# Attention output and expert queries: one block at a time, or two blocks on each weight tile

## The chip, the cores and the metric

The kernel runs on one core of a Trainium2 chip. The metric is device time in microseconds (us). An execution has five engines that run their own instruction lists in order, each list fixed when the kernel is built: TensorE (PE, with its weight loads as PEld), VectorE (DVE), ScalarE (ACT), GpSimd (POOL) and SyncE (SP), whose queue issues almost all plain transfers. Indirect transfers (gathers) are issued by POOL.

## The reference

Two layers over 512 tokens of width 1024, all in f32, with six modulation vectors per layer that are computed from a condition `c`.

```python
for l in range(DEPTH):
    mod = c_act @ ada_w[l] + ada_b[l]                      # [1024] x [1024, 6144]
    sh1, sc1, g1, sh2, sc2, g2 = jnp.split(mod, 6, axis=-1)
    h = _modulate(x, sh1, sc1)
    mix = _hybrid_mixer(h, ...)                            # h @ w_in [1024, 1952], three kinds of heads, @ w_o [1024, 1024]
    x = _layer_norm(alpha * x + (1.0 + g1) * mix, ln1_g[l], ln1_b[l])
    h = _modulate(x, sh2, sc2)
    ffn = _peer(h, peer_wq[l], peer_k1[l], peer_k2[l], peer_u[l], peer_v[l])
    x = _layer_norm(alpha * x + (1.0 + g2) * ffn, ln2_g[l], ln2_b[l])
```

The mixer is causal over the tokens: a block of 128 tokens attends to itself and to the blocks ahead of it. `_peer` multiplies h by `wq` [1024, 2048], scores the result against two sets of 128 keys in each of 8 heads, takes the best 16 of each set, the best 16 of the 256 sums, and so 128 experts of 16384 for each token. Each expert is a row of 1024 in `u_tab` and one in `v_tab`: `out = sum(g * gelu(u . h) * v)`.

## The kernel before, in words

The tokens are four blocks of 128 (0 to 3). A layer has two stages.

**Attention stage.** For each block: `prepare` (layer norm, transpose to `hT`), `project` (times w_in, for a pair of blocks at once), `attend` (the three kinds of heads, result `cat`), `output` (times w_o, result `rt`), `between` (row operations with the modulation rows, layer norm, the new residual `xs`, the second modulation `h2d`, its transpose `h2T`), `queries` (times peer_wq in four groups of 512 columns; for each group a copy, transposes `ptq`, key scores `pms`, a copy `scs`, and the best 16 on DVE, L617 to L622), and `pick`, which ends in the expert numbers `eidx` (L669). The weight products all go through `gemm` (L149 to L162). A weight tile `wt` is 512 KB: four row groups of 128 by 256 columns. SP issues its load when one of 3 or 4 buffers is free. `output` and `queries` are called for one block, so w_o and peer_wq are read four times a layer. `project` is called for (0, 1) and (2, 3), so w_in is read twice.

In the order of the code, blocks 0 and 1 go through attend, output, between, queries and pick one after the other. `project` of (2, 3) is held behind the last query matmul of block 0 (`behind`). Block 2 then attends; the second half of its queries stands behind block 3's attention.

`ada_side` computes the modulation vectors beside layer 0's attention: 20 groups of 512 columns, each from 256 KB tiles `adw` in three buffers. For the first eight groups DVE multiplies and adds (L207, L209); for the last twelve, half of the columns goes over ACT (L203) and POOL (L205). A small matmul `adp` (L211) sums each half over the partitions.

**Expert stage.** For blocks 1 and 2 all experts are computed: the tables u and v are streamed through PE in full (`dense`), after DVE and PE have built a matrix G from the picks of both blocks (`build`, DVE lines L788 to L797, PE L804). Blocks 0 and 3 gather their own experts (`experts`): POOL issues a gather of 128 rows, 512 KB, and DVE multiplies it, L696 and L698 for u, L708 and L713 for v. Four gather buffers exist, so a gather waits until DVE is done with the gather four before. `EARLY` gathers, 80 in layer 0 and 110 in layer 1, have no place ordered for them; they may go out as soon as block 0 has its `eidx`. The later gathers are tied to steps of the build and of the dense loop. Four more go out with the first build steps, so 84 and 114 gathers are issued ahead of the build. The last 50 of layer 0 stand in layer 1's attention.

A list scheduler sets the order of each engine's instructions when the kernel is built, from a model of their times. So a late instruction on an engine holds all that stands behind it there.

## Time and profile before

| | |
|---|---|
| median of three runs | 3564.16 us (3544.61 to 3568.53) |
| the profiled execution | 3550.53 us, of which the span is 3548.8 us |
| busy: PE, DVE, POOL, ACT | 87%, 78%, 42%, 26% of the span |
| moved by DMA | 1012.14 MB, 285 GB/s on the mean |
| granted TensorE clock, mean | 0.927 of full speed |
| layer 0: attention stage until the first build step | 0 to 676.1 us |
| layer 1: attention stage until the first build step | to 2427.1 us |

The dense stage takes the rest: from 676.1 to about 1780 us, and from 2427.1 us to the end. In f32 each matmul is two records in the trace. The weight loads are 128 of peer_wq, 64 of w_o and 56 of w_in, of up to 512 KB each. Rows that name L157 are the matmuls of `gemm`; h2T, cat or hT beside it tells whether they belong to queries, output or projection.

### The profile page before, as it was taken

The numbers are of one execution on the slowest core, as the hardware profiler recorded it, in microseconds if no ns is written. First come the engines' busy times: TensorE is split into PE (matmuls) and PEld (weight loads), VectorE is DVE, ScalarE is ACT, GpSimd is POOL, SyncE is SP. The second block draws the span as 40 slices with busy tenths as digits, with TensorE's granted clock in tenths as the row PEclk, the third lists the DMA queues.
The fourth block names the chain that finished last, engine by engine and source line by source line (L and its number), as shares of the span: only waits on it lengthen the run. The fifth ranks groups of instructions, "written<-read, shape, count | busy, mean of one in ns | idle before, by whom it ended". The sixth has DMA issues, their size and how long they took to land.

```text
span 3548.8 us, 54489 instructions
## 1 busy us (share of the span) xinstructions
PE 3072.0 (87%) x19708; PEld 2258.0 (64%) x19708; DVE 2765.7 (78%) x6277; ACT 927.4 (26%) x1860; POOL 1476.2 (42%) x1347
## 2 busy tenths in 40 slices
PE   7889768658999999999948896776699999999998
PEld 4657536536777776777736774555467767777775
DVE  4668996999777877776675579889998778776777
ACT  2342432222222222222222223312222222222221
POOL 1025573256343334444462045534454434444543
PEclk9989889859999999999979996997699999999998
DMA  9777978568898888899986586885789988989997
GB/s 276 221 230 251 313 261 287 174 187 282 306 322 307 316 310 310 311 348 344 337 288 206 173 292 211 296 294 178 238 275 350 333 312 316 331 323 335 358 353 256
DMA packets 430173, 1012.14 MB, mean 285 GB/s; under 512 B 40504, under 2 KB 229192, under 8 KB 429904
## 3 DMA queue, kind: packets, MB, share of 16 engines
q0 software_dynamic: 147456, 536.94, 42.5%
q1 hardware_dynamic: 282448, 471.73, 39.6%
q8 instruction: 156, 2.56, 0.3%
q14 instruction: 113, 0.93, 0.1%
HBM read 1002.06 MB, written 6.34 MB: 284 GB/s over the span
## 4 chain that ended last, share of the span: by engine, by line
PE 13%; DVE 13%; DMA 10%; issue 9%; POOL 4%; ACT 1%; SPq 0%; POOLq 0%; DVEq 0%; ACTq 0%
DMA g<-in_peer_v,eidx 5%; PE pm L157 4%; PE acc L849 3%; DVE acc L713 2%; POOL g L696 2%; DVE g L698 2%; DMA g<-in_peer_u,eidx 2%; DVE tk_ef L668 1%; PE sp L831 1%; PE sp L832 1%; PE sp L833 1%; PE utp L817 1%; DMA wt<-in_peer_wq 1%; POOL g L708 1%; DVE o L797 1%
## 5 line engine op out<-in xcount | busy, mean ns | idle before, releaser
L708 POOL DMA_INDIRECT g<-in_peer_v,eidx x512 | 613.4, 1198 | 782.0 <-DVE acc L713 481.7
L849 PE MATMUL acc<-v,ge 128*128 128x512 f32 x2048 | 928.9, 595 | 6.4 <-DVE ge L837 5.8
L696 POOL DMA_INDIRECT g<-in_peer_u,eidx x512 | 603.2, 1178 | 764.4 <-DVE g L698 499.9
L713 DVE SCALAR_TENSOR_TENSOR acc<-g,wts,acc 128x1024 f32<-128x1024 f32 x508 | 674.2, 1327 | 145.1 <-DMA g<-in_peer_v,eidx 137.7
L698 DVE SCALAR_TENSOR_TENSOR g<-g,h 128x1024 f32<-128x1024 f32 x512 | 620.3, 1225 | 172.9 <-DMA g<-in_peer_u,eidx 161.8
L831 PE MATMUL sp<-hh,uh 128*128 128x256 f32 x2048 | 613.7, 300 | 1.6 <-ACT ge L835 0.9
L849 PEld LDWEIGHTS acc<-v,ge 128*128 128x128 f32 x2048 | 370.3, 190 | 370.7 <-issue 364.1
L833 PE MATMUL sp<-hh,ul 128*128 128x256 f32 x2048 | 594.8, 290 | 0.0
L832 PE MATMUL sp<-hl,uh 128*128 128x256 f32 x2048 | 583.7, 285 | 0.0
L819 ACT CAST uh<-utp 128x512 fp32r<-128x512 f32 x512 | 304.1, 595 | 871.9 <-PE utp L817 710.9
L821 DVE TENSOR_TENSOR ul<-utp,uh 128x512 fp32r<-128x512 f32 x512 | 347.6, 684 | 110.5 <-ACT uh L819 104.2
L831 PEld LDWEIGHTS sp<-hh,uh 128*128 128x128 f32 x2048 | 392.4, 192 | 7.6 <-issue 5.5
L832 PEld LDWEIGHTS sp<-hl,uh 128*128 128x128 f32 x2048 | 392.1, 191 | 5.3 <-issue 5.3
L833 PEld LDWEIGHTS sp<-hh,ul 128*128 128x128 f32 x2048 | 391.4, 191 | 0.1
L817 PE MATMUL utp<-ident,u 128*128 128x128 f32 x2048 | 302.9, 277 | 49.0 <-DVE ul L821 46.5
L817 PEld LDWEIGHTS utp<-ident,u 128*128 128x128 f32 x2048 | 236.4, 142 | 126.9 <-issue 70.7
L806 ACT COPY G<-pg 128x344 f32<-128x344 f32 (+1 forms) x192 | 146.8, 765 | 593.9 <-PE pg L804 477.5
L804 PEld LDWEIGHTS <-o 128*128 128x128 bf16 x4608 | 163.3, 102 | 187.4 <-issue 91.9
L804 PE MATMUL pg<-o,o 128*128 128x43 bf16 (+1 forms) x4608 | 183.9, 190 | 104.7 <-DVE o L797 86.4
L157 PE MATMUL pm<-wt,h2T 128*128 128x256 f32 x1024 | 235.9, 385 | 17.6 <-DMA wt<-in_peer_wq 16.7
L157 PE MATMUL pm<-wt,hT 128*128 128x256 f32 (+1 forms) x1024 | 232.4, 380 | 12.6 <-ACT hT L274 6.3
L157 PEld LDWEIGHTS pm<-wt,h2T 128*128 128x128 f32 x1024 | 193.3, 193 | 51.0 <-DMA wt<-in_peer_wq 21.5
(235 smaller groups left out, 3448.2 us busy)
## 6 DMA issues: line engine op xcount, KB each, us to landing
u<-in_peer_u SPq DMA_DIRECT2D x256, 512.0 KB
v<-in_peer_v SPq DMA_DIRECT2D x256, 512.0 KB
wt<-in_peer_wq SPq DMA_DIRECT2D x128, 512.0 KB
adw<-in_ada_w SPq DMA_DIRECT2D x160, 256.0 KB
wt<-in_w_o SPq DMA_DIRECT2D x64, 512.0 KB
wt<-in_w_in SPq DMA_DIRECT2D x56, 512.0 KB
wt<-in_ada_w SPq DMA_DIRECT2D x16, 512.0 KB
g<-in_peer_u,eidx POOLq DMA_INDIRECT x512
```

The source lines that it names most:

```text
L157: r = nc.tensor.matmul(pm[:, c0:c0 + m], lhsT=lhsT[:, k0 + k, :], rhs=wt[:, k, :m], start=k0 + k == 0, stop=k0 + k == KT - 1)
L696: nc.gpsimd.indirect_dma_start(out=g, out_offset=None, in_=u_flat, in_offset=bass.IndirectOffsetOnAxis(ap=eidx[:, h, k:k + 1], axis=0))
L698: after(nc.vector.scalar_tensor_tensor(out=g, in0=g, scalar=1.0, in1=h2, op0=OP.mult, op1=OP.mult, accum_out=dots[:, h, k:k + 1]))
L708: nc.gpsimd.indirect_dma_start(out=g, out_offset=None, in_=v_flat, in_offset=bass.IndirectOffsetOnAxis(ap=eidx[:, h, k:k + 1], axis=0))
L713: r = nc.vector.scalar_tensor_tensor(out=acc, in0=g, scalar=wts[:, h, k:k + 1], in1=acc, op0=OP.mult, op1=OP.add)
L804: nc.tensor.matmul(pg[:, tt, 0:n], lhsT=o2[:, tt // TI, :, tt % TI], rhs=o1a[:, tt // TI, p, 0:n, tt % TI], start=tt == 0 and p == 0, stop ...
L817: nc.tensor.transpose(pt[:, j * P:(j + 1) * P], u[:, k * P:(k + 1) * P], ident)
L821: nc.vector.tensor_tensor(ul.rearrange("p j t -> p (j t)"), pt, uh.rearrange("p j t -> p (j t)").bitcast(F32), op=OP.subtract)
L831: nc.tensor.matmul(sp, lhsT=uh[:, j, :], rhs=hh[:, k, :], start=k == 0, stop=False)
L832: nc.tensor.matmul(sp, lhsT=uh[:, j, :], rhs=hl[:, k, :], start=False, stop=False)
L833: nc.tensor.matmul(sp, lhsT=ul[:, j, :], rhs=hh[:, k, :], start=False, stop=k == KT - 1)
L849: nc.tensor.matmul(acc[i][g], lhsT=w[:, i * P:(i + 1) * P], rhs=v[:, g * 512:(g + 1) * 512], start=a == 0, stop=a == NK - 1)
```

## The change

`gemm` takes tiles of two row groups by 512 columns instead of four by 256; a tile stays 512 KB, and a row of it in memory is 2 KB instead of 1 KB. `output` and `queries` take a list of two blocks, and each tile serves both. So w_o is loaded 32 times instead of 64 and peer_wq 64 instead of 128, 48 MB less in all. The products are the same. The order of the stage changes with it: both blocks of a pair attend, then comes one output for both, the two `between`, one `queries` for both, and the two picks. `project` of (2, 3) is held behind the last query matmul of blocks 0 and 1. The pick of block 2 follows the queries of blocks 2 and 3. `ada_side` works on tiles of 128 by 512, and DVE's operations there are 512 columns wide for the first eight groups. Buffers: weight tiles of layer 0 from 4 + 3 to 3 + 3, of layer 1 from 4 + 4 to 4 + 3; the tiles `rt`, `h2d`, `h2T` from 2 to 3; the transposes and scores of the queries take their PSUM tiles from the tag of the transposes ("tr").

```diff
--- before.py
+++ after.py
@@ -35,12 +35,11 @@
...
-WK = 4
-ADK = 2
+WK = 2
...
-BUFS = (dict(w=4, wp=3, scs=1), dict(w=4, wp=4, scs=2))
+BUFS = (dict(w=3, wp=3, scs=1), dict(w=4, wp=3, scs=2))
@@ -147,18 +146,16 @@
...
     def gemm(src, n, lhsTs, pms, tag, behind=None):
-        for c0 in range(0, n, 256):
-            m = min(256, n - c0)
-            for k0 in range(0, KT, WK):
-                wt = A.w.tile([P, WK, 256], F32, name="wt", tag=tag, bufs=A.bufs[tag])
-                nc.sync.dma_start(wt[:, :, :m], src[k0 * P:(k0 + WK) * P, c0:c0 + m].rearrange("(k p) n -> p k n", p=P))
-                for lhsT, pm in zip(lhsTs, pms):
-                    for k in range(WK):
-                        r = nc.tensor.matmul(pm[:, c0:c0 + m], lhsT=lhsT[:, k0 + k, :], rhs=wt[:, k, :m],
-                                             start=k0 + k == 0, stop=k0 + k == KT - 1)
-                        if behind is not None:
-                            order(r, behind)
-                            behind = None
+        for k0 in range(0, KT, WK):
+            wt = A.w.tile([P, WK, 512], F32, name="wt", tag=tag, bufs=A.bufs[tag])
+            nc.sync.dma_start(wt[:, :, :n], src[k0 * P:(k0 + WK) * P, :].rearrange("(k p) n -> p k n", p=P))
+            for lhsT, pm in zip(lhsTs, pms):
+                for k in range(WK):
+                    r = nc.tensor.matmul(pm[:, :n], lhsT=lhsT[:, k0 + k, :], rhs=wt[:, k, :n],
+                                         start=k0 + k == 0, stop=k0 + k == KT - 1)
+                    if behind is not None:
+                        order(r, behind)
+                        behind = None
         return r
...
     def ada_side(l, groups):
         for g in groups:
             t = A.ad.tile([P, 512], F32, name="adt", bufs=1)
-            for c0 in range(0, 512, 256):
-                tt = t[:, c0:c0 + 256]
-                for q in range(0, KT, ADK):
-                    wt = A.ad.tile([P, ADK, 256], F32, name="adw", bufs=3)
-                    nc.sync.dma_start(wt, ada_w[l, q * P:(q + ADK) * P, g * 512 + c0:g * 512 + c0 + 256]
-                                      .rearrange("(k p) n -> p k n", p=P))
-                    for k in range(ADK):
-                        ck = cact[:, q + k:q + k + 1]
-                        if l and c0 == 0:
-                            w = tt if q == 0 and k == 0 else wt[:, k, :]
-                            nc.scalar.activation(w, wt[:, k, :], AF.Copy, scale=ck)
-                            if q or k:
-                                nc.gpsimd.tensor_tensor(tt, tt, w, op=OP.add)
-                        elif q == 0 and k == 0:
-                            nc.vector.tensor_scalar(tt, wt[:, k, :], ck, None, op0=OP.mult)
-                        else:
-                            nc.vector.scalar_tensor_tensor(tt, wt[:, k, :], ck, tt, op0=OP.mult, op1=OP.add)
+            for k in range(KT):
+                wt = A.ad.tile([P, 512], F32, name="adw", bufs=3)
+                nc.sync.dma_start(wt, ada_w[l, k * P:(k + 1) * P, g * 512:(g + 1) * 512])
+                ck = cact[:, k:k + 1]
+                m = 256 if l else 0
+                if m:
+                    w = t if k == 0 else wt
+                    nc.scalar.activation(w[:, 0:m], wt[:, 0:m], AF.Copy, scale=ck)
+                    if k:
+                        nc.gpsimd.tensor_tensor(t[:, 0:m], t[:, 0:m], wt[:, 0:m], op=OP.add)
+                if k == 0:
+                    nc.vector.tensor_scalar(t[:, m:], wt[:, m:], ck, None, op0=OP.mult)
+                else:
+                    nc.vector.scalar_tensor_tensor(t[:, m:], wt[:, m:], ck, t[:, m:], op0=OP.mult, op1=OP.add)
...
-    def output(y, b, cat):
+    def output(y, cats):
         l = y.l
-        rt = A.work.tile([P, D], F32, name="rt", tag="tok", bufs=2)
+        rts = [A.work.tile([P, D], F32, name="rt", tag="tok", bufs=3) for _ in cats]
         for c0 in range(0, D, 512):
-            pm = A.ps.tile([P, 512], F32, name="pm", tag="mm", bufs=2)
-            gemm(w_o[l, :, c0:c0 + 512], 512, [cat], [pm], "w")
-            nc.scalar.copy(rt[:, c0:c0 + 512], pm)
-        return rt
+            pms = [A.ps.tile([P, 512], F32, name="pm", tag="mm", bufs=2) for _ in cats]
+            gemm(w_o[l, :, c0:c0 + 512], 512, cats, pms, "w")
+            for rt, pm in zip(rts, pms):
+                nc.scalar.copy(rt[:, c0:c0 + 512], pm)
+        return rts
...
-        h2 = A.work.tile([P, D], F32, name="h2d", tag="tok", bufs=2)
+        h2 = A.work.tile([P, D], F32, name="h2d", tag="tok", bufs=3)
...
-    def queries(y, h2T, v1, fi, groups):
+    def queries(y, hs):
         l = y.l
-        for g in groups:
-            pm = A.ps.tile([P, 512], F32, name="pm", tag="mm", bufs=2)
-            r = gemm(peer_wq[l, :, g * 512:(g + 1) * 512], 512, [h2T], [pm], "w")
...
+        for g in range(4):
+            pms = [A.ps.tile([P, 512], F32, name="pm", tag="mm", bufs=2) for _ in hs]
+            r = gemm(peer_wq[l, :, g * 512:(g + 1) * 512], 512, [h[0] for h in hs], pms, "w")
+            qs = []
+            for pm in pms:
+                q = A.work.tile([P, 512], F32, name="q", tag="q", bufs=2)
+                nc.scalar.copy(q, pm)
+                qs.append(q)
+            for q, (_, v1, fi) in zip(qs, hs):
+                pt = A.ps.tile([P, 512], F32, name="ptq", tag="tr", bufs=2)
+                for m in range(4):
...
+                kT = A.work.tile([P, 4, P], F32, name="qkT", tag="qkT", bufs=1)
...
+                pm = A.ps.tile([P, 4, NK], F32, name="pms", tag="tr", bufs=2)
...
+                top16([(v1[:, 4 * g + m, :], i1[:, m, :], scs[:, m, :]) for m in range(4)])
+                nc.vector.tensor_copy(fi[:, 2 * g:2 * g + 2].rearrange("p h a k -> p (h a) k"), i1)
         return r
@@ -914,31 +912,26 @@
         if l + 1 < L:
             ada_side(0, range(4, 12))
         layer_rows(y)
-        behind = None
         for p in ps:
-            b = p[0]
             attend(y, *p)
-            if b == 1:
-                for b2 in (2, 3):
-                    prepare(y, b2)
-            h = between(y, b, output(y, b, p[2]))
-            r = queries(y, *h, range(4))
-            if b == 0:
-                behind = r
+        for b in (2, 3):
+            prepare(y, b)
+        rts = output(y, [p[2] for p in ps])
+        hs = [between(y, b, rt) for b, rt in zip((0, 1), rts)]
+        behind = queries(y, hs)
+        for b, h in zip((0, 1), hs):
             res[b] = pick(b, *h[1:])
-        p2, p3 = project(y, (2, 3), behind)
+        ps = project(y, (2, 3), behind)
         if l + 1 < L:
             ada_side(1, range(12))
-        attend(y, *p2)
-        h = between(y, 2, output(y, 2, p2[2]))
-        queries(y, *h, range(2))
-        attend(y, *p3)
-        rt = output(y, 3, p3[2])
-        queries(y, *h, range(2, 4))
-        res[2] = pick(2, *h[1:])
-        h = between(y, 3, rt, lambda: A.ps.tile([P, 512], F32, name="prow", tag="at", bufs=2))
-        queries(y, *h, range(4))
-        res[3] = partial(pick, 3, *h[1:])
+        for p in ps:
+            attend(y, *p)
+        rts = output(y, [p[2] for p in ps])
+        mk = lambda: A.ps.tile([P, 512], F32, name="prow", tag="at", bufs=2)
+        hs = [between(y, b, rt, mk) for b, rt in zip((2, 3), rts)]
+        queries(y, hs)
+        res[2] = pick(2, *hs[0][1:])
+        res[3] = partial(pick, 3, *hs[1][1:])
```

Where the change moves instructions: PE in layer 0, at the end of the queries of the first block. In these rows `pm<-wt,h2T` are query matmuls, `pm<-wt,hT` is the projection of blocks 2 and 3, `pm<-wt,cat` the output of block 1, `ptq` and `pms` the transposes and scores of the queries, `prow` the modulation rows of a `between`. Before:

```order
L157 MATMUL pm<-wt,h2T 128x256 x12
L211 MATMUL adp<-adt,nones 1x512
L157 MATMUL pm<-wt,h2T 128x256 x4
L157 MATMUL pm<-wt,hT 128x256 x11
L601 MATMUL ptq<-ident,q 128x128 x4
L157 MATMUL pm<-wt,hT 128x256 x5
L157 MATMUL pm<-wt,hT 128x160 x6
L606 MATMUL pms<-keysT,qkT 128x128 x4
L157 MATMUL pm<-wt,cat 128x256 x16
L157 MATMUL pm<-wt,hT 128x160 x4
L157 MATMUL pm<-wt,cat 128x256 x8
L227 LDWEIGHTS sel
```

The projection, the output of block 1 and its `between` stand mixed with the queries. With the change, at the start of the queries of blocks 0 and 1:

```order
L220 MATMUL prow<-rows_159,sel 128x256
L258 MATMUL pt<-ident,h2d 128x128 x8
L204 MATMUL adp<-adt,nones 1x512
L154 MATMUL pm<-wt,h2T 128x512 x12
L204 MATMUL adp<-adt,nones 1x512
L154 MATMUL pm<-wt,h2T 128x512 x4
L599 MATMUL ptq<-ident,q 128x128 x4
L154 MATMUL pm<-wt,h2T 128x512 x8
L604 MATMUL pms<-keysT,qkT 128x128 x4
L599 MATMUL ptq<-ident,q 128x128 x4
L154 MATMUL pm<-wt,h2T 128x512 x4
```

Here all `prow` and both transposes of h2d stand ahead of the first query matmul, and no `hT` or `cat` matmul stands among the queries; the projection follows as a whole behind the last of them.

POOL in layer 0, around block 2's `between`: `ve` and `rs_r` are the two small steps of a layer norm on POOL, two pairs for each `between`; L696 and L708 (L694 and L706 with the change) are block 0's gathers. Before:

```order
L708 DMA g<-in_peer_v,eidx_1674 128x1024
L205 TENSOR_TENSOR adt<-adt,adw 128x256
L708 DMA g<-in_peer_v,eidx_1674 128x1024 x3
L248 TENSOR_SCALAR ve<-bnmv 128x1
L237 TENSOR_TENSOR rs_r<-ve,mhalf 128x1
L708 DMA g<-in_peer_v,eidx_1674 128x1024 x3
L248 TENSOR_SCALAR ve<-bnmv 128x1
L237 TENSOR_TENSOR rs_r<-ve,mhalf 128x1
L708 DMA g<-in_peer_v,eidx_1674 128x1024
L696 DMA g<-in_peer_u,eidx_1674 128x1024
L205 TENSOR_TENSOR adt<-adt,adw 128x256 x3
L696 DMA g<-in_peer_u,eidx_1674 128x1024
```

The `between` of block 2 stands among the last of the first 32 v gathers; the next 20 u gathers and block 3's `between` follow. With the change, at the same place:

```order
L706 DMA g<-in_peer_v,eidx_1943 128x1024 x2
L665 TENSOR_TENSOR tk_pick<-tk_hot,tk_ce 128x400
L706 DMA g<-in_peer_v,eidx_1943 128x1024 x29
L694 DMA g<-in_peer_u,eidx_1943 128x1024 x20
L241 TENSOR_SCALAR ve<-bnmv 128x1
L230 TENSOR_TENSOR rs_r<-ve,mhalf 128x1
L241 TENSOR_SCALAR ve<-bnmv 128x1
L230 TENSOR_TENSOR rs_r<-ve,mhalf 128x1
L241 TENSOR_SCALAR ve<-bnmv 128x1
L230 TENSOR_TENSOR rs_r<-ve,mhalf 128x1
L241 TENSOR_SCALAR ve<-bnmv 128x1
L230 TENSOR_TENSOR rs_r<-ve,mhalf 128x1
```

All 84 gathers now stand ahead of the two `between` of blocks 2 and 3. In layer 1 it is the same with 114.

## Rows read from the trace of the kernel before

**Rows 1.** the page, part 1: busy us, share of the span, instructions

```profile
PE 3072.0 (87%) x19708; PEld 2258.0 (64%) x19708; DVE 2765.7 (78%) x6277; ACT 927.4 (26%) x1860; POOL 1476.2 (42%) x1347
```

**Rows 2.** stretches: length, busy us (instructions) by engine, clock, DMA share, GB/s

```profile
0.00:50.00 50.00, 34.19 (x136) 12.82 (x136) 17.57 (x59) 7.94 (x8) 9.53 (x22) 0.97 1.00 300
...
200.00:210.00 10.00, 4.26 (x11) 1.63 (x11) 10.00 (x21) 1.35 (x3) 1.64 (x4) 0.50 0.25 80
...
210.00:220.00 10.00, 10.00 (x51) 7.84 (x52) 4.40 (x9) 9.63 (x26) 3.28 (x6) 0.78 0.45 142
...
350.00:400.00 50.00, 45.78 (x218) 34.76 (x216) 44.69 (x178) 16.86 (x38) 23.78 (x25) 1.00 1.06 374
...
450.00:500.00 50.00, 34.79 (x116) 20.23 (x114) 47.23 (x62) 13.65 (x28) 38.72 (x37) 0.80 0.73 235
...
650.00:700.00 50.00, 28.39 (x286) 24.55 (x287) 48.03 (x166) 14.92 (x27) 14.17 (x15) 0.80 0.41 141
...
1500.00:1700.00 200.00, 200.00 (x1115) 145.05 (x1115) 139.99 (x193) 43.84 (x85) 89.53 (x77) 1.00 0.94 347
```

**Rows 3.** lines 0 to 690 us: count, busy us, mean ns, idle before, releasers

```profile
L157 PE MATMUL pm<-wt,h2T 128*128 128x256 f32 x512 | 118.1, 386 | 7.9 <-DMA wt<-in_peer_wq 7.6 <-issue 0.4
...
L157 PE MATMUL pm<-wt,hT 128*128 128x256 f32 (+1 forms) x512 | 116.7, 381 | 10.6 <-ACT hT L274 6.3 <-DMA wt<-in_w_in 2.9 <-ACT lat L385 0.9
...
L157 PE MATMUL pm<-wt,cat 128*128 128x256 f32 x256 | 65.1, 408 | 12.5 <-DMA wt<-in_w_o 10.2 <-ACT cat L531 1.4 <-ACT rt L571 0.6
...
L698 DVE SCALAR_TENSOR_TENSOR g<-g,h 128x1024 f32<-128x1024 f32 x51 | 63.5, 1248 | 15.2 <-DMA g<-in_peer_u,eidx 11.7 <-issue 3.4
...
L713 DVE SCALAR_TENSOR_TENSOR acc<-g,wts,acc 128x1024 f32<-128x1024 f32 x31 | 47.0, 1515 | 0.1
...
L668 DVE TENSOR_REDUCE tk_ef<-tk_pick 128x8 f32<-128x400 f32 x48 | 41.3, 862 | 3.8 <-POOL tk_pick L667 3.8
...
L665 DVE TENSOR_TENSOR tk_hot<-iotaj,tk_tib 128x400 bf16<-128x400 bf16 x48 | 19.8, 413 | 0.2
```

**Rows 4.** chain that ended last, layer 1, weight waits: start, us, what

```profile
2084.10 16.46 DMA wt<-in_peer_wq
...
2210.93 4.87 DMA wt<-in_w_o
...
2233.66 7.74 DMA wt<-in_w_o
...
2290.80 16.89 DMA wt<-in_peer_wq
...
2328.83 11.94 DMA wt<-in_w_o
```

**Rows 5.** one line each: durations (ns), first and last start (us)

```profile
L577 DVE SCALAR_TENSOR_TENSOR rt<-xs,rt x4: 1214/1226/1227, 190.5 to 601.3; 128x1024 f32<-128x1024 f32 x4
...
L577 DVE SCALAR_TENSOR_TENSOR rt<-xs,rt x4: 1204/1222/1226, 1955.2 to 2345.9; 128x1024 f32<-128x1024 f32 x4
...
L669 DVE CAST eidx<-tk_ef x3: 212/219/227, 327.9 to 667.7; 128x128 int32<-128x128 f32 x3
...
L669 DVE CAST eidx<-tk_ef x3: 216/226/227, 2068.9 to 2413.1; 128x128 int32<-128x128 f32 x3
...
L788 DVE TENSOR_TENSOR o<-iotab,i2T x4: 678/680/681, 676.1 to 686.5; 128x1024 bf16<-128x1024 bf16 x4
...
L788 DVE TENSOR_TENSOR o<-iotab,i2T x4: 680/682/691, 2427.1 to 2437.7; 128x1024 bf16<-128x1024 bf16 x4
...
L211 PE MATMUL adp<-adt,nones x16: 590/590/591, 52.0 to 167.6; 128*1 128x512 f32 x16
```

**Rows 6.** timeline of PE, first query matmuls of block 0: start, us

```profile
216.46 5.78 PE L157 MATMUL pm<-wt,h2T 128*128 128x256 f32 x26
...
1976.42 2.86 PE L157 MATMUL pm<-wt,h2T 128*128 128x256 f32 x12 [0.34 <-ACT h2T L267]
```

**Rows 7.** u gathers of layer 1, 2069 to 2155 us: first, last start

```profile
L696 POOL DMA_INDIRECT g<-in_peer_u,eidx x32: 934/937/1942, 2069.4 to 2152.2; - x32
```

More of the change, by code (lines that the diff above doesn't have):

```diff
@@ L178, in ada_first @@
             pm = A.ps.tile([P, 512], F32, name="pm", tag="mm", bufs=2)
-            for c0 in range(0, 512, 256):
-                for k0 in range(0, KT, WK):
-                    tag = "wp" if k0 else "w"
-                    wt = A.w.tile([P, WK, 256], F32, name="wt", tag=tag, bufs=A.bufs[tag])
-                    nc.sync.dma_start(wt, ada_w[0, k0 * P:(k0 + WK) * P, g * 512 + c0:g * 512 + c0 + 256]
-                                      .rearrange("(k p) n -> p k n", p=P))
-                    for k in range(WK):
-                        nc.tensor.matmul(pm[0:1, c0:c0 + 256], lhsT=cact[:, k0 + k:k0 + k + 1], rhs=wt[:, k, :],
-                                         start=k0 + k == 0, stop=k0 + k == KT - 1)
+            for k0 in range(0, KT, WK):
+                tag = "wp" if k0 % 4 else "w"
+                wt = A.w.tile([P, WK, 512], F32, name="wt", tag=tag, bufs=A.bufs[tag])
+                nc.sync.dma_start(wt, ada_w[0, k0 * P:(k0 + WK) * P, g * 512:(g + 1) * 512]
+                                  .rearrange("(k p) n -> p k n", p=P))
+                for k in range(WK):
+                    nc.tensor.matmul(pm[0:1, :], lhsT=cact[:, k0 + k:k0 + k + 1], rhs=wt[:, k, :],
+                                     start=k0 + k == 0, stop=k0 + k == KT - 1)
             ada_finish(0, g, ar, pm)
@@ L578, in between @@
         affine(y, xs[b], rt, rt, 0, 1, mk)
-        h2 = A.work.tile([P, D], F32, name="h2d", tag="tok", bufs=2)
+        h2 = A.work.tile([P, D], F32, name="h2d", tag="tok", bufs=3)
         affine(y, h2, h2, xs[b], 2, 3, mk)
-        h2T = A.work.tile([P, KT, P], F32, name="h2T", tag="tok", bufs=2)
+        h2T = A.work.tile([P, KT, P], F32, name="h2T", tag="tok", bufs=3)
         transpose_cols(h2T, h2, KT, tag="tr" if mk else "mm")
@@ new lines, in queries @@
+        for g in range(4):
[9 more added lines that the diff above has]
+                for m in range(4):
+                    nc.tensor.transpose(pt[:, m * P:(m + 1) * P], q[:, m * P:(m + 1) * P], ident)
+                kT = A.work.tile([P, 4, P], F32, name="qkT", tag="qkT", bufs=1)
+                nc.scalar.copy(kT, pt.rearrange("p (m t) -> p m t", m=4))
+                pm = A.ps.tile([P, 4, NK], F32, name="pms", tag="tr", bufs=2)
+                for m in range(4):
+                    nc.tensor.matmul(pm[:, m, :], lhsT=kT[:, m, :], rhs=y.keysT[:, 4 * g + m, :], start=True, stop=True)
+                scs = A.work.tile([P, 4, NK], F32, name="scs", bufs=A.bufs["scs"])
+                nc.scalar.copy(scs, pm)
+                i1 = topp.tile([P, 4, TOPK], U32, name="tk_i", bufs=2)
+                top16([(v1[:, 4 * g + m, :], i1[:, m, :], scs[:, m, :]) for m in range(4)])
+                nc.vector.tensor_copy(fi[:, 2 * g:2 * g + 2].rearrange("p h a k -> p (h a) k"), i1)
```

17 lines of the change are left out of this document (removed).

## The prediction

> **What bounds the kernel now.** I read the page first: PE is busy for 87% and DVE for 78% of the span [rows 1]. That is an average over stages, so I went on to the busy time of short stretches. In the dense stage PE is at 200 of 200 us with 347 GB/s [rows 2]; neither w_o nor peer_wq is read there, and with the change as many gathers (84 and 114) are issued ahead of the build, so I leave both dense stages as they are. The change works on the attention stages: 676.1 us in layer 0, and in layer 1 up to 2427.1 us, the first build steps [rows 5]. There no engine bounds for long. PE has 45.8 of 50 us at 350 to 400 us, DVE 47.2 at 450 to 500 and 48.0 at 650 to 700, in the build [rows 2]. What keeps them busy is that different blocks are in different steps: block 0's gathers run on DVE while PE projects blocks 2 and 3.
>
> Then I asked what weight loads cost. In the lines of layer 0, PE sat idle for w_o 10.2 us, for peer_wq 7.6 and for w_in 2.9 [rows 3], 20.7 in all. In the chain of waits, layer 1 has five waits for w_o and peer_wq, 16.46 + 4.87 + 7.74 + 16.89 + 11.94 = 57.9 us [rows 4]. That is the most that 48 MB less can give by itself: some 79 us. Last I took the times at which the row operations, the picks and the builds start [rows 5], to see what the new order does to them.
>
> **The sum** goes against the profiled execution, 3550.5 us, which is 13.6 us (0.4%) under the median of 3564.16.
>
> *Layer 0, queries of blocks 0 and 1.* Block 0's row operations begin at 190.5 us [rows 5]. Now they wait for block 1's attention and a shared output. One block's output is 65.1 / 4 = 16.3 us of PE [rows 3]; with what is left of block 1's attention I take 27 us (between 16 and 60), so 217. A `between` takes 26 us here (190.5 to the first query matmul at 216.5) and 21 in layer 1 (1955.2 to 1976.4) [rows 5, 6]. Two of them side by side take between 26 and 52 us; since DVE was at 10.00 of 10 us inside one [rows 2], I take 50: 267. The order shows no PE work to fill this time. The queries of a block are 118.1 / 4 = 29.5 us of matmuls [rows 3], a pair 59. Transposes and scores have a quarter of those columns, some 15 us, of which half lies beside: 68 us, so 335. These matmuls count without weight waits, so the saving on loads is in the sum.
>
> *Block 0's picks.* From its first query matmul (216.5) to its `eidx` (327.9) it was 111.4 us [rows 5, 6]. The 16 picks cost 0.86 + 0.41 us each on DVE [rows 3]; with POOL's product between the two, which I take to be as long as the 0.86, about 35 us. What lies ahead of them is between 0 and 111.4 - 29.5 - 35 = 47; I take 23. `eidx` comes at 335 + 58 = 393 instead of 327.9: **65 us later**, and so do the gathers.
>
> *The 84 gathers.* DVE needs 52 x 1.248 + 32 x 1.515 = 113 us for them [rows 3], and 16 x 1.27 = 20 for block 1's picks: 134 at least. At the pace of layer 1, 32 gathers in 82.8 us, 2.67 each [rows 7], it would be 224. The attention of blocks 2 and 3 uses DVE as well, but less than in those rows; I take 174: 567. PE has these 232 us from 335 for the projection (116.7 / 2 = 58 [rows 3]), two attentions and an output, which covers them.
>
> *From there to the build.* By the order of POOL both `between` of blocks 2 and 3 come behind all 84 gathers. I give 28 us (0 to 33) to what is left of attention and output, 44 to the two `between`, 72 to the queries with the first of their picks: 711, against 676.1. **+35** for layer 0. With every term at its low end it is -79 (`between` -46, gathers -40, rest -28), at its high end about +125 (block 1's attention +33, gathers +50, queries +6).
>
> *Layer 1* goes alike, without modulation work beside it: 1955.2 + 23, two `between` of 21 (2021), queries 66 (2087), picks 53: `eidx` at 2140 instead of 2068.9. Its 114 gathers, 64 u and 50 v, need 156 us of DVE, 176 with picks, up to 304 at 2.67; I take 208, nearer to the low end, since only attention lies beside them: 2348. Then 44 and 70: 2462, against 2427.1. **+35**, between -40 and +130.
>
> *Build.* Block 2's picks, 16 x 1.27 = 20 us of DVE, stood ahead of the first build step; now they stand among the steps, where DVE is at 48 of 50 [rows 2]. Between 0 and 20 a layer; I take 8, **+16** for both.
>
> *Tiles of 2 KB rows.* The first 50 us move 300 GB/s at a DMA share of 1.00, all with 1 KB rows; the dense stage, with 4 KB rows, 347 at 0.94, that is 369 at full share [rows 2]. If 2 KB rows reached the latter, the first loads would end 50 x (1 - 300 / 369) = 9 us sooner; between 0 and 9, I take **-4**. Elsewhere this only shortens loads that the sum counts at nothing. The Trainium skill ("DMA: Bandwidth & Descriptors", Measured) goes by the size of a whole transfer and asks for 1 MiB; tiles stay at 512 KB, so by it this term would be 0.
>
> *Modulation sums with 512 columns, half as many weight loads into PE, fewer buffers:* at nothing. DVE is busy for 17.6 of the first 50 us [rows 2], and PE's weight loads run beside matmuls. With three buffers for 3.46 us of matmuls each, a load has longer than before.
>
> *Clock.* Inside one `between` (200 to 210 us) PE was busy for 4.26 of 10 us and the granted clock was 0.50; in the next 10 us, all busy, 0.78 [rows 2]. So a return to queries costs about 10 x 0.22 = 2.2 us. Before, eight single ones could pay it, now four double ones: 0. The Trainium skill ("TensorE: Matmul & The Clock Gate", HAM oscillation) says that PE falls to the slow clock when it idles between bursts and begins the next burst slow. The row agrees; by that rule each double `between` with an idle PE surely pays, 4 x 2.2 = 9 us more.
>
> 35 + 35 + 16 - 4 = 82; 3550.5 + 82 = **3632 us**.
>
> **The rivals.**
>
> *The loads were the bound (faster).* If DVE catches up, the build starts when PE and its weights are done. All weight waits go, 20.7 + 57.9 = 79: **3472 us**. For it: the five waits stand on the chain itself [rows 4], and DVE's total work is a little less than before. Against it: gathers now begin 65 us later and stand ahead of `between`, and in the chain's remainder they would be waited for. It decides if the gather stretch of layer 0 falls under 140 us, since 711 - 34 is the old 676. Chance 0.22.
>
> *Lost overlap and saved waits cancel (same).* If gathers run at DVE's own pace in both layers, the sum loses 40 + 32 = 72: **3560 us**. For it: in 450 to 500 us DVE was at 94% already [rows 2]. Chance 0.21.
>
> *The modulation loads hold the queries (slower still).* The sums `adp` of all 20 groups now stand in PE's list ahead of the last query groups of blocks 0 and 1. The first eight groups ran from 52.0 to 167.6 us, 16.5 us each [rows 5]; twelve more at that pace end at 167.6 + 198 = 366 instead of 335, +31: **3663 us**. It decides if a group takes over 14 us. Against it: half of the work of the later groups is on ACT and POOL. Chance 0.12.
>
> *Forecast:* 0.45, with a range of its own from 3590 to 3690.
>
> **How the numbers follow.** About 1% is what a measurement of this kernel can tell from no change, so faster means under 3528 us and slower over 3600. Faster: the first rival and a little of the second, 0.24. Same: most of the second and the low edge of the forecast, 0.22. Slower: the rest, 0.54. The range reaches from 3485, inside the first rival, to 3700, past the third; about 0.1 lies under it and 0.08 over it.
>
> **What would show it.** In the changed profile: block 0's first `eidx` at about 393 us and 2140 less the shift; PE nearly idle at a clock of 0.5 for some 45 us in front of the first query matmuls of each pair; the gathers of layer 0 ending near 567, and both `between` of blocks 2 and 3 after that; the first build near 711; no large waits for peer_wq or w_o on the chain. I am wrong if the two `between` overlap so that the pair costs no more than one, if gathers take under 2 us each beside attention, or if the build begins before 676 us.

## The result, and the profile after

The changed kernel takes 3741.43 us (median of four, 3732.06 to 3751.85) against 3566.35 for the kernel before in the same session: a ratio of 1.0515, 95% interval 1.049 to 1.0539. It is 5% slower. The forecast was 3632 us, slower by 2%; the measured time lies outside its range of 3485 to 3700.

The page, first the busy line that answers to [rows 1], then what DMA moved:

```profile
PE 3117.6 (83%) x18364; PEld 2039.4 (55%) x18364; DVE 2778.6 (74%) x6213; ACT 937.1 (25%) x1864; POOL 1472.6 (39%) x1347
...
DMA packets 313938, 961.63 MB, mean 257 GB/s; under 512 B 38968, under 2 KB 51528, under 8 KB 313680
```

PE and DVE are busy for a little longer than before (+46 and +13 us), and 50 MB less are moved. The span is 191 us longer: most of it is idle time on both engines. The stamps that answer to [rows 5] say where (row operations, `eidx`, first build steps; and the first dense matmuls of layer 0, L829):

```profile
L571 DVE SCALAR_TENSOR_TENSOR rt<-xs,rt x4: 1224/1226/1345, 237.9 to 651.5; 128x1024 f32<-128x1024 f32 x4
...
L571 DVE SCALAR_TENSOR_TENSOR rt<-xs,rt x4: 1224/1226/1226, 2089.4 to 2492.9; 128x1024 f32<-128x1024 f32 x4
...
L667 DVE CAST eidx<-tk_ef x3: 196/209/215, 406.7 to 812.5; 128x128 int32<-128x128 f32 x3
...
L667 DVE CAST eidx<-tk_ef x3: 199/214/214, 2232.1 to 2661.6; 128x128 int32<-128x128 f32 x3
...
L786 DVE TENSOR_TENSOR o<-iotab,i2T x4: 673/677/679, 754.2 to 769.4; 128x1024 bf16<-128x1024 bf16 x4
...
L786 DVE TENSOR_TENSOR o<-iotab,i2T x4: 678/678/928, 2595.0 to 2607.7; 128x1024 bf16<-128x1024 bf16 x4
...
L829 PE MATMUL sp<-hh,uh x24: 274/282/579, 819.6 to 841.7; 128*128 128x256 f32 x24
...
L154 PE MATMUL pm<-wt,hT x128: 512/592/1033, 1934.0 to 2000.4; 128*128 128x512 f32 x96, 128*128 128x416 f32 x32
```

The last row is the first projection of layer 1. Before, these two were:

```profile
L831 PE MATMUL sp<-hh,uh x24: 274/281/502, 685.2 to 701.2; 128*128 128x256 f32 x24
...
L157 PE MATMUL pm<-wt,hT x256: 299/379/796, 1825.6 to 1893.4; 128*128 128x256 f32 x112, 128*128 128x160 f32 x16
```

So, from mark to mark: layer 0 until the first build step 754 instead of 676 (+78); from there to layer 1's first projection 1180 instead of 1150 (+30); layer 1's attention stage 661.0 instead of 601.5 (+60); from its build to the end 1145 instead of 1122 (+23). The sum is the 191 us. Stretches of layer 0 (columns as in [rows 2]):

```profile
240.00:250.00 10.00, 2.68 (x10) 0.90 (x8) 9.08 (x21) 2.98 (x7) 5.46 (x8) 0.50 0.55 172
...
270.00:280.00 10.00, 5.05 (x15) 1.88 (x13) 6.31 (x13) 3.86 (x8) 4.47 (x8) 0.50 0.60 187
...
450.00:500.00 50.00, 24.98 (x62) 12.14 (x62) 46.12 (x80) 12.71 (x27) 39.15 (x31) 0.53 0.74 240
...
600.00:650.00 50.00, 39.60 (x141) 18.93 (x140) 14.42 (x22) 10.75 (x19) 1.61 (x4) 0.91 0.24 80
...
650.00:700.00 50.00, 46.35 (x151) 23.82 (x150) 21.12 (x87) 7.82 (x14) 1.58 (x4) 0.95 0.36 120
...
750.00:800.00 50.00, 11.69 (x200) 9.10 (x199) 48.97 (x97) 8.77 (x13) 24.69 (x22) 0.50 0.34 107
```

PE and DVE take turns: at 240 to 280 DVE does the two `between` and PE waits at a granted clock of 0.50, the lower of its two levels (1.2 of 2.4 GHz); at 450 to 500 DVE does gathers and PE is half idle; at 600 to 700 PE finishes output and queries while DVE has 14 and 21 of 50 us to do; at 750 to 800 DVE picks and builds, and PE has 12. In layer 1's chain of waits only two waits for w_o are left of the 57.9 us of [rows 4], and none for peer_wq:

```profile
2061.95 6.04 DMA wt<-in_w_o
...
2469.30 7.15 DMA wt<-in_w_o
```

The weight waits went, and the kernel became slower all the same.

### The profile page after: what moved, and what is told of

It reads as the page before. It is cut to its first block, busy times and chain, and to the rows that moved or that the text cites. A ratio compares the mean times of both kernels' runs of the same rounds, so it can differ in the third digit from the quotient of the medians.

```text
span 3739.6 us, 51743 instructions
## 1 busy us (share of the span) xinstructions
PE 3117.6 (83%) x18364; PEld 2039.4 (55%) x18364; DVE 2778.6 (74%) x6213; ACT 937.1 (25%) x1864; POOL 1472.6 (39%) x1347
## 5 line engine op out<-in xcount | busy, mean ns | idle before, releaser
L706 POOL DMA_INDIRECT g<-in_peer_v,eidx x512 | 624.3, 1219 | 733.5 <-DVE acc L711 461.2
L694 POOL DMA_INDIRECT g<-in_peer_u,eidx x512 | 600.5, 1173 | 685.0 <-DVE g L696 492.6
L711 DVE SCALAR_TENSOR_TENSOR acc<-g,wts,acc 128x1024 f32<-128x1024 f32 x508 | 654.8, 1289 | 168.3 <-DMA g<-in_peer_v,eidx 164.0
L696 DVE SCALAR_TENSOR_TENSOR g<-g,h 128x1024 f32<-128x1024 f32 x512 | 638.0, 1261 | 189.2 <-DMA g<-in_peer_u,eidx 188.5
L829 PE MATMUL sp<-hh,uh 128*128 128x256 f32 x2048 | 615.5, 301 | 3.2 <-ACT ge L833 2.1
L829 PEld LDWEIGHTS sp<-hh,uh 128*128 128x128 f32 x2048 | 394.9, 193 | 9.5 <-issue 4.5
L154 PE MATMUL pm<-wt,hT 128*128 128x512 f32 (+1 forms) x512 | 225.9, 592 | 25.0 <-ACT hT L267 12.9
L154 PE MATMUL pm<-wt,h2T 128*128 128x512 f32 x512 | 234.9, 610 | 3.4 <-DMA wt<-in_peer_wq 3.4
L665 POOL TENSOR_TENSOR tk_pick<-tk_hot,tk_ce 128x400 f32<-128x400 bf16 x128 | 128.9, 1007 | 241.7 <-DVE tk_hot L663 237.2
```

The source lines that it names most:

```text
L154: r = nc.tensor.matmul(pm[:, :n], lhsT=lhsT[:, k0 + k, :], rhs=wt[:, k, :n], start=k0 + k == 0, stop=k0 + k == KT - 1)
L694: nc.gpsimd.indirect_dma_start(out=g, out_offset=None, in_=u_flat, in_offset=bass.IndirectOffsetOnAxis(ap=eidx[:, h, k:k + 1], axis=0))
L696: after(nc.vector.scalar_tensor_tensor(out=g, in0=g, scalar=1.0, in1=h2, op0=OP.mult, op1=OP.mult, accum_out=dots[:, h, k:k + 1]))
L706: nc.gpsimd.indirect_dma_start(out=g, out_offset=None, in_=v_flat, in_offset=bass.IndirectOffsetOnAxis(ap=eidx[:, h, k:k + 1], axis=0))
L711: r = nc.vector.scalar_tensor_tensor(out=acc, in0=g, scalar=wts[:, h, k:k + 1], in1=acc, op0=OP.mult, op1=OP.add)
L829: nc.tensor.matmul(sp, lhsT=uh[:, j, :], rhs=hh[:, k, :], start=k == 0, stop=False)
```

## The experiments

Each is compared with the kernel before on its own chip; the ratio is what is compared between them, with its interval. "No tag" below means that ptq and pms take their PSUM tiles from mm, as before the change.

**Parts of the change together (e1 to e4).** My theory was that the order of the pairs is the whole loss. e1 calls `output` and `queries` of the changed kernel for one block at a time, in the order before:

```diff
...
-        rts = output(y, [p[2] for p in ps])
-        hs = [between(y, b, rt) for b, rt in zip((0, 1), rts)]
-        behind = queries(y, hs)
...
+            h = between(y, b, output(y, [p[2]])[0])
+            r = queries(y, [h])
...
```

> The changed kernel's tiles (two row groups by 512 columns), its modulation loads and its buffers, but output and queries for one block at a time and in the order of the kernel before; w_o and peer_wq are read four times a layer again. If the loss of 175 us lies in the order of the stage (theory), this takes 3566 us within 1% (3530 to 3600). If it lies in the shape of the tiles, in the three buffers or in the modulation loads (rival), it takes over 3630.

Measured 3688.5 us, 1.0397 (1.0371 to 1.0422). **My theory fell**: without any pair most of the loss was still there. e2 and e3 restore the old order for blocks 2 and 3, or for 0 and 1, alone:

> As the changed kernel, but only blocks 0 and 1 go as a pair; blocks 2 and 3 as in the kernel before. Theory (each pair costs its own overlap): 50 to 100 us over the kernel before, since block 0's picks still come some 55 to 80 us later in each layer, less what the mixed order of blocks 2 and 3 makes up. Rival (only both pairs together cost, because gathers pile up ahead of blocks 2 and 3): under 30 us over it. Rival (the first pair alone is the loss): over 140.

> As the changed kernel, but only blocks 2 and 3 go as a pair; blocks 0 and 1 as in the kernel before. Theory: 70 to 120 us over the kernel before, because the two between, the shared queries and the picks of both blocks stand behind all gathers and nothing runs beside them. With e2, the two excesses add up to about 175. Rival (the late picks of block 0 are the loss): under 30 us over it.

Measured 3694.72 us, 1.0418 (1.0397 to 1.044), and 3730.0 us, 1.0536 (1.05 to 1.0571). The excesses add up to far more than 175 us: something else is in all of them. e4 keeps the order and gives each block its own loads:

```diff
+    def gemm_own(src, n, lhsTs, pms, tag):
+        for k0 in range(0, KT, WK):
+            for lhsT, pm in zip(lhsTs, pms):
+                wt = A.w.tile([P, WK, 512], F32, name="wt", tag=tag, bufs=A.bufs[tag])
...
-            gemm(w_o[l, :, c0:c0 + 512], 512, cats, pms, "w")
+            gemm_own(w_o[l, :, c0:c0 + 512], 512, cats, pms, "w")
...
```

> The changed kernel's order, but each block of a pair loads its own tiles of w_o and peer_wq: 64 and 128 loads as before the change. Theory (the saved 48 MB lie beside matmuls in this order): within 25 us of the changed kernel, 3741. Rival (the saved loads are worth what the waits for them were, and hide part of a still larger loss): 60 to 90 us over it, near 3810.

Measured 3764.07 us, 1.0616 (1.0586 to 1.0646), against 1.0515 for the changed kernel. By the ratios, sharing the loads in this order is worth about 1.0% or 36 us, more than I said and less than the rival; by the bare medians, which come from two chips, it is 23 us, within what I said.

**One part at a time on the kernel before (e5 to e8).** e5 moves two PSUM tiles (the buffers that matmuls write to; tiles of one tag share the number of buffers in `bufs`, here two):

```diff
-            pt = A.ps.tile([P, 512], F32, name="ptq", tag="mm", bufs=2)
+            pt = A.ps.tile([P, 512], F32, name="ptq", tag="tr", bufs=2)
...
-            kT = A.work.tile([P, 4, P], F32, name="qkT", tag="q", bufs=2)
+            kT = A.work.tile([P, 4, P], F32, name="qkT", tag="qkT", bufs=1)
...
-            pm = A.ps.tile([P, 4, NK], F32, name="pms", tag="mm", bufs=2)
+            pm = A.ps.tile([P, 4, NK], F32, name="pms", tag="tr", bufs=2)
```

> The kernel before with one thing of the change: the transposes and scores of the queries (ptq, pms) take their PSUM tiles from the tag tr instead of mm, and qkT has a buffer of its own. The run with the changed tiles and buffers in the old order took 141 us more than the kernel before, so the order of the pairs is not the main loss. Theory A (the shared PSUM tag makes queries and the transposes of projection and attention wait for each other): 60 to 140 us over the kernel before. Theory B (the tiles of 2 x 512): under 20 us over it. Theory C (any new time in the scheduler's model gives another list, and the old one was an unusually good one): 40 us or more here and in each of the next three.

e6 takes over `gemm`, `ada_first` and `WK = 2`; e7 takes over `ada_side`; e8 takes over `BUFS` and three buffers of the tag tok.

> The kernel before with only gemm and the first modulation loads on tiles of two row groups by 512 columns. Buffers, PSUM tags, modulation loads beside the attention and the order are as before. Theory A: within 20 us of the kernel before. Theory B (the tiles): 60 to 140 us over it. Theory C: 40 or more over it, with the loss in gathers, projection and attention that stand in another order.

> The kernel before with only the modulation loads beside the attention changed: tiles of 128 by 512, DVE's operations 512 columns wide for the first eight groups. Theory A and B: within 20 us of the kernel before, possibly 10 faster since DVE has half as many operations there. Theory C: 40 or more over it.

> The kernel before with only the buffers of the change: weight tiles 3 + 3 in layer 0 and 4 + 3 in layer 1, three buffers for rt, h2d and h2T. Theory A and B: within 20 us of the kernel before (slower by at most the wait for one load in flight less). Theory C: 40 or more over it.

| | median us | ratio, interval |
|---|---|---|
| e5, PSUM tag | 3715.95 | 1.0481, 1.0457 to 1.0505 |
| e6, tiles | 3538.73 | 0.9976, 0.996 to 0.9992 |
| e7, modulation loads | 3557.75 | 1.0033, 1.001 to 1.0056 |
| e8, buffers | 3557.08 | 1.0036, 1.0018 to 1.0054 |

Theory A holds in kind: a tag that moves no data and no work costs 168 us, more than the 60 to 140 that I gave, while tiles, modulation loads and buffers are within 0.4%. Theory C, a list that is worse after any change, falls with those three. The trace of e5 shows how. These are the transposes of the softmax in the attention of blocks 0 and 1 (L522, tag tr), by stretches: PE busy, PEld busy, clock, DMA. Before:

```profile
170.00:200.00 30.00, 2.84 (x16) 1.87 (x16) 0.96 0.76 230
...
250.00:300.00 50.00, 0.00 (x0) 0.00 (x0) 1.00 0.84 264
```

and with the tag, followed by the weight loads of the scores `pms` of block 0's queries:

```profile
170.00:200.00 30.00, 0.00 (x0) 0.00 (x0) 0.82 0.73 230
...
250.00:300.00 50.00, 3.37 (x16) 2.38 (x16) 0.76 0.43 134
...
L606 PEld LDWEIGHTS pms<-keysT,qkT x32: 186/192/192, 229.1 to 256.8; 128*128 128x128 f32 x32
```

Before, block 1's transposes (16 records) were done by 194 us, ahead of block 0's queries. With the tag they come after the last `pms` of block 0 (256.8). Both now draw on two buffers of one tag, and block 0's queries stand ahead of block 1's attention in the code, so attention waits for the queries to give the buffers back; in PE's list the transposes stand behind the scores. In this code, which takes blocks one by one, a tag decides which blocks may overlap. That qkT's own buffer is not the cause is shown by e12 below, which has it too.

**The pairs without the tag (e9 to e12).** Each is the changed kernel, or e2, e3, e1, with this edit:

```diff
-                pt = A.ps.tile([P, 512], F32, name="ptq", tag="tr", bufs=2)
+                pt = A.ps.tile([P, 512], F32, name="ptq", tag="mm", bufs=2)
...
-                pm = A.ps.tile([P, 4, NK], F32, name="pms", tag="tr", bufs=2)
+                pm = A.ps.tile([P, 4, NK], F32, name="pms", tag="mm", bufs=2)
```

> The changed kernel with one thing undone: ptq and pms of the queries take their PSUM tiles from mm again. In the old order the tag alone cost 168 us, because block 1's attention, whose transposes use tr and stand later in the code, had to wait for block 0's queries. Theory D (pairing and the tag remove the same overlap of one block's attention with another's queries; where the pairs have already removed it the tag is free): within 30 us of the changed kernel, 3700 to 3760. Rival E (the tag is the whole loss and the pairs cost nothing): 3600 or less.

> Tiles, modulation loads and buffers of the change, blocks 0 and 1 as a pair, blocks 2 and 3 one by one, ptq and pms in mm. With tr it took 3695 us. Theory D: blocks 2 and 3 overlap again, the first pair does not: 3590 to 3660. Rival E: 3560 or less.

> As the run before, but blocks 2 and 3 are the pair and 0 and 1 go one by one. With tr it took 3730 us. Theory D: blocks 0 and 1 overlap again, and the end of the stage does not: 3600 to 3670. Rival E: 3560 or less.

> All of the change without the pairs and without the tag: tiles, modulation loads and buffers, one block at a time, ptq and pms in mm. Singly these three were at -9, +10 and +10 us. Theories D and E: within 25 us of the kernel before, 3525 to 3575. If it is over 3600, the parts cost together what none of them costs alone, and neither theory holds.

| order | tag tr | no tag |
|---|---|---|
| one by one | e1 3688.5, 1.0397 | e12 3531.47, 0.9938 (0.9914 to 0.9962) |
| pair (0, 1) | e2 3694.72, 1.0418 | e10 3643.45, 1.0258 (1.0231 to 1.0285) |
| pair (2, 3) | e3 3730.0, 1.0536 | e11 3664.17, 1.0311 (1.0287 to 1.0334) |
| both pairs | changed kernel 3741.43, 1.0515 | e9 3758.79, 1.0564 (1.0535 to 1.0593) |

All four came as theory D says. Without the tag, the first pair costs 112 us over e12, the second 133, both 227: nearly the sum. By the ratios, the tag costs 4.6% where blocks go one by one (some 163 us), 1.6% and 2.2% where one pair is left (57 and 80), and nothing where both are pairs (there the kernel with the tag is even 0.5% lower). So pairs and tag take away the same thing. That it is a block's attention beside another's queries I read from the code and from the trace of e5. e12 is faster than both kernels, by 0.6% than the one before: the other parts of the change cost nothing together. The idle time of DVE shows the loss; before, the changed kernel, e5 and e12, one row each (100 us; PE, PEld, DVE, ...):

```profile
550.00:650.00 100.00, 83.86 (x413) 64.46 (x412) 76.11 (x341) 20.16 (x36) 25.39 (x25) 0.97 0.82 266
```

```profile
550.00:650.00 100.00, 76.14 (x285) 40.80 (x285) 41.32 (x72) 29.86 (x57) 21.01 (x21) 0.84 0.42 142
```

```profile
550.00:650.00 100.00, 76.00 (x344) 52.10 (x343) 50.61 (x141) 27.52 (x53) 23.56 (x21) 0.89 0.56 188
```

```profile
550.00:650.00 100.00, 87.62 (x307) 43.28 (x306) 69.74 (x321) 23.22 (x42) 20.85 (x23) 0.95 0.74 246
```

The changed kernel and e5 leave DVE idle for half of this stretch. But a fixed stretch lies at different steps in different kernels (e17 below, slow as well, has DVE busy for 78.8 of these 100 us), so the whole way from 150 us to the first build step of layer 0 says more:

| | length, us | PE busy | DVE busy | DVE idle | clock |
|---|---|---|---|---|---|
| before | 526 | 413 | 427 | 99 | 0.90 |
| e12 | 528 | 420 | 416 | 112 | 0.89 |
| e5 | 620 | 441 | 432 | 188 | 0.84 |
| changed kernel | 604 | 446 | 406 | 198 | 0.81 |
| e9 | 626 | 453 | 407 | 219 | 0.81 |

DVE does about the same work in all five; what the slow ones add is idle time.

**What carries the cost (e13 to e17).** e13 takes the bytes alone from the kernel before:

```diff
+    def gemm_half(src, n, lhsTs, pms, tag):
...
+                nc.sync.dma_start(wt[:, 0:2, :m], src[k0 * P:(k0 + 2) * P, c0:c0 + m].rearrange("(k p) n -> p k n", p=P))
...
+                        r = nc.tensor.matmul(pm[:, c0:c0 + m], lhsT=lhsT[:, k0 + k, :], rhs=wt[:, k % 2, :m],
...
-            gemm(w_o[l, :, c0:c0 + 512], 512, [cat], [pm], "w")
+            gemm_half(w_o[l, :, c0:c0 + 512], 512, [cat], [pm], "w")
...
```

> The kernel before, in which each tile of w_o and peer_wq is loaded only by half (256 KB), and the second half of its matmuls uses the first half's rows again: 48 MB less, the same instructions and about the same order; the products of output and queries are computed with half of the weights. Theory F (loads were never the bound: waits for weights move to other waits): within 25 us of the kernel before. Rival G (the weight waits of 79 us were real): 3470 to 3500.

Measured 3541.95 us, 0.999 (0.9974 to 1.0006): nothing. The waits of layer 1's chain are 9.3 us instead of 57.9:

```profile
1937.90 2.72 DMA wt<-in_w_o
...
2337.09 6.56 DMA wt<-in_peer_wq
```

Theory F holds, and the forecast's first rival falls: waits for weights on the chain are replaced by others there (those for u gathers grow from 1.6% to 3.7% of the span). This holds for the order before; in the order of the change e4 found the same bytes to be worth about 1%. e14 orders the first build step behind block 2's `eidx`:

```diff
...
+            if ch == 0 and t0 == 0:
+                order(r0, lastpick[2])
...
```

> The changed kernel with block 2's 16 picks ordered ahead of the first build step, as they stood before the change. In the changed kernel the first dense matmul comes 65 us behind the first build step, before it was 9. If the picks among the build steps cost (theory H): 15 to 50 us under the changed kernel. If DVE has the same work either way (rival): within 10 us of it.

Measured 3737.81 us, 1.054 (1.0514 to 1.0566), the same as the changed kernel. The first build step of layer 0 comes 29 us later:

```profile
L788 DVE TENSOR_TENSOR o<-iotab,i2T x5: 685/687/689, 783.3 to 789.9; 128x1024 bf16<-128x1024 bf16 x5
```

The stretch from there to layer 1's first projection is shorter by 44 us (1136 instead of 1180), in an execution that was the fastest of four (3724.11). DVE has its work either way. e15 sets `EARLY = (32, 32)` in the changed kernel, e16 in the kernel before:

> The changed kernel with EARLY = (32, 32): 48 and 78 gathers fewer stand ahead of the two between of blocks 2 and 3; they go to the dense stage. Theory I (those gathers hold attention, between and the build): 60 to 170 us under the changed kernel, measured against what the same cut does to the kernel before in the next run. Rival (PE's own sequence without overlap sets the stage): within 30 us of the changed kernel, or slower.

> The kernel before with EARLY = (32, 32), the control of the run before. The attention stages have fewer gathers, the dense stages more. Theory I: within 40 us of the kernel before, since here gathers lie beside PE's work; both signs are possible.

Measured 3753.24 us, 1.0575 (1.0538 to 1.0611), and 3559.77 us, 1.0037 (1.002 to 1.0054). First build steps of layer 0, e15 and then e16:

```profile
L786 DVE TENSOR_TENSOR o<-iotab,i2T x16: 671/679/1590, 720.5 to 785.2; 128x1024 bf16<-128x1024 bf16 x16
```

```profile
L788 DVE TENSOR_TENSOR o<-iotab,i2T x36: 678/686/693, 654.9 to 777.3; 128x1024 bf16<-128x1024 bf16 x36
```

Fewer gathers shorten layer 0's stage by 34 us in e15 and by 21 in the control, and the time as a whole falls in neither. Theory I falls: the gathers ahead of the two `between` are not what the pairs cost. e17 lets the projection of blocks 2 and 3 go in e9:

```diff
-        ps = project(y, (2, 3), behind)
+        ps = project(y, (2, 3))
```

> The changed kernel with ptq and pms in mm (3759 us in that form), and the projection of blocks 2 and 3 no longer held behind the last query matmul of blocks 0 and 1: in PE's list it now stands among the output and the two between of blocks 0 and 1. Theory J (the first pair costs because project of blocks 2 and 3 begins 90 us later and with it all that follows): the first build step of layer 0 comes 30 to 70 us sooner than the 777 of that form, and the time is 3640 to 3720. Rival K (what is lost is the overlap of attention with queries, whatever stands in front): within 25 us of 3759.

Measured 3703.03 us, 1.0405 (1.0369 to 1.0442), 56 us under e9. Its `eidx` and first build steps of layer 0, and below them the same two lines of e9:

```profile
L667 DVE CAST eidx<-tk_ef x2: 208/212/217, 471.8 to 559.2; 128x128 int32<-128x128 f32 x2
...
L786 DVE TENSOR_TENSOR o<-iotab,i2T x12: 676/677/680, 736.8 to 788.9; 128x1024 bf16<-128x1024 bf16 x12
...
L667 DVE CAST eidx<-tk_ef x2: 200/207/214, 425.2 to 510.6; 128x128 int32<-128x128 f32 x2
...
L786 DVE TENSOR_TENSOR o<-iotab,i2T x2: 680/680/681, 776.7 to 777.3; 128x1024 bf16<-128x1024 bf16 x2
```

The build comes 40 us sooner than in e9 although block 0's `eidx` comes 47 us later. Theory J holds for that part: the late projection is about a quarter of e9's 206 us. The other 150 us I put down to one thing: while two blocks share a tile, neither can attend beside the other's queries. That the order of the pairs costs these us is shown by e9 to e12; that it does so through this overlap is argued from the idle time above, and no run divides them among the steps of the stage.

## Why the prediction was wrong

**The direction was right, and so was the mechanism as far as it went: picks, gathers and builds come later because a pair has nothing beside its `between`. The size was not.** The sum had +82; measured were +191 from profile to profile. Its terms, for layer 0 and layer 1:

| step of the sum | forecast | measured |
|---|---|---|
| layer 0, first row operation of blocks 0 and 1 | 217 | 237.9 |
| both `between`, to their first query matmul | 50 (267) | 42 (280.1) |
| their queries | 68 | 72.4 |
| block 0's `eidx` | 393 | 406.7 |
| the 84 gathers, first to last | 174 | 178 |
| what is left of attention and output | 28 | 54 (to block 2's row operation, 638.3) |
| `between`, to the first query matmul | 44 | 12 |
| queries of blocks 2 and 3 | 72 | 72 |
| from there to the first build step | 0 | 32 |
| layer 1, block 0's `eidx`, from the first projection | 314 | 298 |
| the 114 gathers | 208 | 240 |
| what is left of attention and output | 0 | 8 (to 2479.9) |
| `between`, to the first query matmul | 44 | 12 |
| queries of blocks 2 and 3 | 70 | 74 |
| from there to the first build step | 0 | 29 |
| builds to the next mark, both layers | +16 | +53 |

The rows behind the gathers, the end of the output of blocks 2 and 3, and DVE's best-16 steps at 720 to 760 us:

```profile
L694 POOL DMA_INDIRECT g<-in_peer_u,eidx x52: 935/959/1990, 407.2 to 583.5; - x52
...
L706 POOL DMA_INDIRECT g<-in_peer_v,eidx x50: 935/941/1987, 2308.6 to 2471.4; - x50
...
L154 PE MATMUL pm<-wt,cat x52: 592/592/697, 595.8 to 638.0; 128*128 128x512 f32 x52
...
L617 DVE FIND_INDEX8 tk_i<-tk_v,scs 128x8 uint32<-128x128 f32 x27 | 7.3, 283 | 0.0
L615 DVE MAX8 tk_v<-scs 128x8 f32<-128x128 f32 x24 | 5.3, 277 | 3.6 <-ACT scs L606 3.6
```

1. *"I give 28 us (0 to 33) to what is left of attention and output"* failed. I had said that PE's 232 us beside the gathers cover the projection, two attentions and an output. The two attentions had no price in my sum. They did not fit: between 407 and 640 us PE waited 17.7 us for DVE's `rsn` and 8.3 for its `qtok`, both in the projection, and 14.5 and 9.9 for ACT's `pr` and `pT` in attention. It had a granted clock of 0.53 at 450 to 500 us, and block 2's row operation, which waits for the output, began only at 638.3. Measured 54.
2. *"72 to the queries with the first of their picks"* failed in its second half. Both blocks' best-16 steps now end together, and DVE needed 32 and 29 us behind the last query matmul before a build could start. My sum counted the matmuls and nothing behind them.
3. *"I take 8"* for block 2's picks among the build steps, with 20 as the upper bound, was too small: +30 and +23. In layer 0, 14 of the 16 picks ran behind the first build step, 17 us of DVE, and 14 of block 0's u gathers beside them; the first dense matmul came 65 us behind that step instead of 9. e14 shows that it is no matter of place. What the bound of 20 left out is not shown.
4. *The `between`* were sized the other way: block 2's queries start after one of them, so a pair costs 12 us there in both layers instead of 44, less than a single one did before at the front of the stage (26 and 21). That was one of my signs of being wrong, but it worked for the kernel and not against it.
5. *The 114 gathers:* 240 instead of 208, since a gather beside attention took 2.1 us, between the two rates that I had named.

What I left out of the sum cost nothing either way here: the PSUM tag. I put "fewer buffers" at nothing and did not price the tag at all. e5 shows 168 us for it in the old order. In the order of the change it is free, so the miss does not come from that; but there were two ways into the same loss, each costly alone, and I had named one.

**The rivals.** *The loads were the bound* is shown false by e13, and the chain of waits misled here: 57.9 us of waits on the chain were worth nothing, as others came in their place. Its own sign, a gather stretch under 140 us in layer 0, did not come either (178). *The modulation loads hold the queries:* the 20 groups ran at 15.4 us each, over the 14 that I gave as its condition,

```profile
L204 PE MATMUL adp<-adt,nones x40: 590/591/1061, 39.3 to 331.6; 128*1 128x512 f32 x40
...
280.10 4.25 PE L154 MATMUL pm<-wt,h2T 128*128 128x512 f32 x6
```

but the last sum came at 331.6 us and not at 366. The queries took 72.4 us, 4 more than forecast, and PE waited 8.4 us at these sums between 250 and 460 us (4.6 and 3.8): the condition came true, the price of 31 did not. *Lost overlap and saved waits cancel* needed the gathers at DVE's own pace, 134 and 176 us; they took 178 and 240. Nor was there a saving to cancel with in the order before (e13); in the new order it is the 36 us of e4.

**Small terms.** The first 50 us now move 308 GB/s at a share of 0.96, that is 321 at full share against 300 with 1 KB rows:

```profile
0.00:50.00 50.00, 32.16 (x74) 6.67 (x74) 22.55 (x66) 7.94 (x8) 10.04 (x24) 1.00 0.96 308
```

and the last matmul on the first modulation loads starts at 44.9 us instead of 49.7, so the -4 was about right. (I had taken all of these loads for 1 KB rows; 2 of the 15 MB are the tokens, with rows of 4 KB, the same in both kernels.) The Trainium skill ("DMA: Bandwidth & Descriptors", Measured) goes by the size of the whole transfer alone, on transfers that GpSimd issues. By that these loads, which SP issues at the same size as before, would have had no change; the measured rate differs by 7%.

The clock, at 0 in the sum, added busy time. It was 0.50 through both `between`, with PE busy for 2.7 and 5.1 of 10 us (rows at 240 and 270 above). The Trainium skill ("TensorE: Matmul & The Clock Gate", HAM oscillation) has the slow clock for a PE that idles between bursts. The rows agree. On the way to layer 0's build the mean fell from 0.90 to 0.81, and attention's matmuls became longer. These are its scores until 690 us before, and until 760 us after:

```profile
L504 PE MATMUL sc<-kT,qT 100*128 100x128 f32 (+3 forms) x64 | 23.9, 482 | 0.7 <-ACT pr L510 0.7
...
L497 PE MATMUL sc<-kT,qT 100*128 100x128 f32 (+3 forms) x64 | 34.1, 658 | 7.0 <-ACT pr L503 3.2 <-DVE sbe L548 2.7 <-ACT v L482 1.2
```

How much of this lengthened the stage is not shown. The query matmuls of layer 0 are as long as before in sum, 118.0 us in half as many records [rows 3], so there half of the weight loads bought nothing, as forecast; those of the output took 57.9 us instead of 65.1 and those of the projection 114.3 instead of 116.7:

```profile
L154 PE MATMUL pm<-wt,h2T 128*128 128x512 f32 x256 | 118.0, 612 | 3.4 <-DMA wt<-in_peer_wq 3.4
```

## What to carry to other kernels

A tile that two blocks share makes the two blocks meet; before sharing, take the bytes alone away (half of each load, same work) and see whether they are worth anything. Where one engine works on one block while another works on the next, what counts is which steps may stand beside which: a buffer tag that two steps share ties them together as firmly as the order of the code, and should be given to steps that follow each other anyway. A stage's sum needs the last engine's tail too: what stands behind the last matmul, for all blocks that end together.
